# Another order of the experts beside a second block's context, and its stores and input loads on GpSimd's queue

## The chip, the cores and the metric

The kernel runs on one core of a Trainium2 chip. The time is the device time of one execution in microseconds; lower is better.

## The reference

Two blocks stand one behind the other. The first is a hybrid layer on 256 tokens of 1024 features (short convolution, stick-breaking attention and forgetting attention side by side) followed by a mixture of experts: 32 experts, 4 for each token. The second block has two layers (neighbourhood attention, gated linear attention and grouped-query attention, then a feed-forward network) on the 256 tokens of the first block's output and on 256 tokens of a context, which doesn't depend on the first block. All is fp32.

```
logits = (xt @ router_w + router_b).astype(jnp.float32)
top_vals, top_idx = lax.top_k(logits, TOP_K)          # 4 of 32
...
u = xt @ w1 + b1                                       # 1024 -> 2048
glu = jnp.minimum(u[:, ::2], SWIGLU_LIMIT)
lin = jnp.clip(u[:, 1::2], -SWIGLU_LIMIT, SWIGLU_LIMIT)
a = glu * jax.nn.sigmoid(SWIGLU_ALPHA * glu) * (lin + 1)
out = a @ w2 + b2                                      # 1024 -> 1024
return acc + gate_e[:, None] * out.astype(jnp.float32), None
```

## The kernel before

After the first block's mixers and router the kernel sorts the experts by the number of their tokens. A **rank** is a place in that order. A rank has a fixed capacity of rows (`CAPS`, L48): 128 for ranks 0 and 1, 64 for ranks 2 to 17, 32 for ranks 18 to 31. Every expert loads 12 MB of weights, as 12 loads of 1 MB into `m_raw` (5 buffers), all issued by SP at L113: 8 for its first layer (`first`, fp32 matmuls at L904) and 4 for its second (`second`, L962). SP issues the loads in the order of the list `order`, so layer 1 of the next rank is loaded ahead of layer 2 of this one. Between the two layers stand the swiglu (L914 to L921) and a transpose (L929); behind the second, the rows are scattered to the tokens (L1012). `UNITS` (L51) groups ranks whose rows are gathered together (`held`, L845, and `inward`, L863), two groups ahead at a time (`prepare`, L1027).

Beside the experts runs a second stream of work, the **side**. It is a generator: first the rest of the first block's ada layer (L242), then `context` (L1588), which takes the 256 context tokens through the part of the second block that they need: projections, attention (`attend`), the states of the gated linear attention (`gla_states`, which end in sf and sb, L1771) and its output (`gla`), then more projections, the FFN, a norm, and the projections and states of layer 2. Its matmuls run as three passes (L195, L196, L197) on weights split into w_hi (ACT, L96) and w_lo (GpSimd or VectorE, L98); its weights, 0.5 MB apiece, come as `w_raw` over ACT's queue. Its PSUM tiles are named c, two buffers. Tensors that the last part needs are stored to memory by `keep` (L1597), and the context itself is loaded twice as x (L1637, L1642). These stores and loads are issued by SP.

How much of the side stands beside which expert is set while the program is written. The expert loop yields its capacity six times for each rank, and `along` (L1887) gives the side a credit and takes steps of it until the credit is used; the costs of attention and GLA steps are multiplied by `DRY`:

```
SHARE = {128: 0.8, 64: 1.45, 32: 3.2}
DRY = 2.0
...
for step in b.experts(keep):
    b.along(SHARE[step] if step else 1e9)
...
def along(self, c):
    self.credit += c
    while self.credit > 0:
        d = next(self.side, None)
```

After the last expert, `last` runs the second block on the 256 tokens of the first block's output.

Of the kernel before, what the change touches and what calls it, by code (L numbers as in the profile page):

```python
# [17 lines left out]
ALU = mybir.AluOpType  # L18
# [7 lines left out]
NE = 32  # L26
# [11 lines left out]


SHARE = {128: 0.8, 64: 1.45, 32: 3.2}  # L40
DRY = 2.0
FILL = 0.8

FIRST = 2
# [3 lines left out]
CAPS = ((0, 2), 128), ((2, 18), 64), ((18, 32), 32)  # L48
CAP = [n for (lo, hi), n in CAPS for _ in range(lo, hi)]

UNITS = [(u,) for u in range(2)] + [(u, u + 1) for u in range(2, 18, 2)] + [tuple(range(u, min(u + 4, NE))) for u in range(18, NE, 4)]  # L51
FC = 22

MIXED = 2, 3, 4, 5, 0, 1, 6, 7
# [77 lines left out]
class Build:  # L132
# [673 lines left out]
    def experts(self, keep):  # L806
# [3 lines left out]
        nc, tc, io = self.nc, self.tc, self.io  # L810
        with tc.tile_pool(name="m1", bufs=1) as p, tc.tile_pool(name="m2", bufs=2) as p2, \
# [4 lines left out]
            x = keep["x1"]  # L816
# [7 lines left out]
            bl = p.tile([P, 192], F32R, name="bl")  # L824
# [20 lines left out]
            def held(rows, ranks):  # L845

                for t in range(2):
                    for e, r in enumerate(ranks):
                        n = CAP[r]
                        nc.vector.tensor_scalar(rows[:, t, e * n:(e + 1) * n], keep["place"][:, 0:n], keep["rslot"][:, t, r:r + 1],  # L850
                                                None, op0=ALU.is_equal)
# [137 lines left out]
            def biases():  # L989

                for k in range(0, KC, 2):
                    po = ps.tile([P, 512], F32, name="m")
                    for i in range(2):
                        c = (k + i) % 4 * P
                        nc.tensor.matmul(po[:, i * T:(i + 1) * T], b2[k // 4][:, c:c + P], gateT, start=True, stop=True)
                    add(k, po)
                    if k == 2:
                        yield
# [18 lines left out]

            reg = [expert(r) for r in range(NE)]

            order = [(r, layer) for r in (0, 1) for layer in (1, 2)] + [(2, 1)]  # L1020
            for r in range(2, NE):
                order += [(r + 1, 1)] * (r + 1 < NE) + [(r, 2)]
            for r, layer in order:
                w.plan(weights(reg[r], layer), False)
            ready = {}
# [1 line left out]
            def prepare(i):  # L1027

                rows = p2.tile([P, 2, 2 * P], F32R, name="rows", tag="glu", bufs=1)
                xT = p2.tile([P, KC, 2 * P], F32, name="xT", bufs=1)  # L1030
                at = 0
                for ranks in UNITS[i:i + 2]:
                    held(rows[:, :, at:], ranks)
                    for r in ranks:
                        ready[r] = xT[:, :, at:at + CAP[r]]
                        at += CAP[r]

                for z in range(at, 2 * P, 64):
                    nc.vector.tensor_copy(rows[:, :, z:z + 64], rows[:, :, at - 64:at])
                inward(rows, xT)  # L1040


            for c in range(2):
                b1 = p2.tile([P, 512], F32, name="b1", tag="yh")
                nc.scalar.dma_start(b1, io["b_mlp1"][c])
                nc.scalar.activation(b1h[:, c], b1, AF.Copy)
                for q in (slice(32, 64), slice(96, 128)):
                    nc.vector.tensor_tensor(b1h[q, c], b1[q], b1h[q, c].bitcast(F32), op=ALU.subtract)
            prepare(0)
            self.all(rank)  # L1050
            pr.__exit__(None, None, None)
            behind = biases()
            unit = {r: i for i, ranks in enumerate(UNITS) for r in ranks}
            aTs, inside, ys = {}, {}, {}
            for n, (r, layer) in enumerate(order):
                m, ranks = CAP[r], UNITS[unit[r]]
                run = first(m, ready[r], chosen(m, perm[:, r:r + 1])) if layer == 1 else second(m, aTs.pop(r))
# [45 lines left out]
            with tc.tile_pool(name="past", bufs=1) as pf, tc.If(most > 0):  # L1103
# [4 lines left out]
                place = pf.tile([P, 2, P], F32, name="placef")  # L1108
# [8 lines left out]
                with tc.For_i(0, NE, 1) as i:  # L1117
# [12 lines left out]
                    for v in range(2):  # L1130
                        with tc.If(past > v * P):
                            after = w.apart([a for layer in (1, 2) for a in weights(lambda: expert_id, layer)])
# [15 lines left out]
                            u = end(first(128, xT, chosen(128, col[:, 4:5])))  # L1148
# [439 lines left out]
    def context(self, w, ps, tag, saved):  # L1588


        nc, tc, io = self.nc, self.tc, self.io
        one = lambda n: tc.tile_pool(name=n, bufs=1, side="right")
        two = lambda n: tc.tile_pool(name=n, bufs=2, side="right")

        def keep(l, name, t):
            saved[l][name] = tc.dram_tile(list(t.shape), F32, name=f"kept_{name}_{l}")
            nc.sync.dma_start(saved[l][name], t)  # L1597

        def halves(pu):
            return [pu.tile([P, KC, T], F32R, name=n) for n in ("uh", "ul")]  # L1600

        def mixers(l, u, pu, full):
            y = None
            with one("cg") as pg:
                o = {n: pg.tile(sh, F32, name=n) for n, sh in self.GLA_SHAPES + (self.FULL_SHAPES[2:] if full else ())}
                with one("cq") as pq:
                    o.update({n: pq.tile(sh, F32, name=n) for n, sh in self.SHAPES + (self.FULL_SHAPES[:2] if full else ())})
                    done = set()
                    with two("cp") as p2:
                        yield from self.projections(l, 1, u, o, w, p2, ps, tag, full, done)  # L1610
                    for n, _ in self.SHAPES:
                        keep(l, n, o[n])
                    if full:
                        y = halves(pu)
                        with two("ca") as p2:
                            yield from dry(self.attend(self.units(l, 1, o, None, done), *y, p2, ps, tag, done))
                with one("cl1") as p, two("cl2") as p2:
                    for n in ("sf", "sb"):
                        o[n] = p.tile([P, 64], F32, name=n)
                    yield from dry(self.gla_states(o, p2, ps, tag))  # L1620
                    for n in ("sf", "sb"):
                        keep(l, n, o[n])
                    if full:
                        yield from dry(self.gla(l, 1, o, None, *y, p, p2, ps, tag, done))
            return y

        def dry(steps):

            for c in steps:
                yield c and c * DRY  # L1630

        mod = [m[:, 1] for m in self.mod2]
        with one("cu") as pu:
            u = halves(pu)
            with one("cx") as px, two("ct") as p2:
                x = px.tile([P, KC, T], F32, name="x")
                nc.sync.dma_start(x, io["ctx"])  # L1637
                yield from self.modulated(x, mod[0][:, 0:8], mod[0][:, 8:16], u, p2)
            y = yield from mixers(0, u, pu, True)
            with one("cx") as px:  # L1640
                x = px.tile([P, KC, T], F32, name="x")
                nc.sync.dma_start(x, io["ctx"])  # L1642
                for k in range(0, KC, 2):
                    nc.gpsimd.tensor_scalar(x[:, k:k + 2], x[:, k:k + 2], ALPHA, None, op0=ALU.mult)
                for i in range(2):
                    with one("cf") as p:
                        acc = p.tile([P, KC, T], F32, name="acc")
                        if i == 0:
                            for ks in MIXED2:
                                yield from self.columns(acc, lambda k: (y[0][:, k], y[1][:, k]), ks, MIXED2[0][0], MIXED2[-1][1], w, ps, tag)  # L1650
                        else:
                            u = halves(pu)
                            with one("ch") as p1, two("ch2") as p2:
                                yield from self.modulated(x, *self.affine(mod[0], 1, 0, 0, p1), u, p2, None, normed)
                                self.settle(x, normed[0], 0, 0, p1)
                                yield from self.ffn(u, w, acc, p1, p2, ps, tag)
                        with two("cr2") as p2:
                            chunk, finish = self.norm(acc, mod[0][:, 24 * i + 16:24 * i + 24], x, px, p2, ps, tag)
                            for k in range(KC):
                                chunk(k)  # L1660
                                yield 0.4
                            normed = finish()
                            yield 1.8
                u = halves(pu)
                with two("ct") as p2:
                    yield from self.modulated(x, *self.affine(mod[1], 0, 0, 1, px), u, p2, None, normed)
                yield from mixers(1, u, pu, False)
# [410 lines left out]
```

## Time and profile before

| | |
|---|---|
| median of three runs | 2369.41 us (2366.2 to 2372.82) |
| profiled execution | 2358.65 us, span 2357.0 us |
| TensorE busy | 2144.4 us, 91% of the span |
| VectorE, ScalarE, GpSimd busy | 46%, 37%, 24% |
| moved by DMA | 667.36 MB, mean 283 GB/s |
| expert stretch | about 279 to 1587 us |

The span is that of one profiled execution; the median is of other executions. Busy time is the time in which an engine works on an instruction, without issuing. The DMA share of a stretch is the mean busy share of the core's 16 DMA engines.

### The profile page before, as it was taken

What the parts mean: (1) busy time and instruction counts of PE and PEld (TensorE: products, weight loads), DVE (VectorE), ACT (ScalarE), POOL (GpSimd) and SP (SyncE); (2) the same over time, 40 slices, a digit from 0 to 9 for tenths busy, and PEclk for the clock granted to TensorE, in tenths of its full rate; (3) what the DMA queues carried; (4) which work ended last, traced back from release to release, by engine and by line L of the source; (5) the groups of instructions that cost most, each with busy time, mean ns of one, the idle gap of its engine ahead of it and who ended that gap; (6) DMA issues with size and microseconds to landing.
All of it is one profiled execution on the core that took longest, in us unless ns stands there. A gap on an engine that the chain in (4) does not pass through costs nothing. (4 is left out here: it accounts for less than half of the span.)

```text
span 2357.0 us, 38285 instructions
## 1 busy us (share of the span) xinstructions
PE 2144.4 (91%) x15238; PEld 1503.0 (64%) x15239; DVE 1087.7 (46%) x2146; ACT 862.6 (37%) x1585; POOL 567.6 (24%) x335
## 2 busy tenths in 40 slices
PE   7899799999999988977999998968989999899998
PEld 4667533455444433524776765637879997788997
DVE  4765333221334322325443345227569767757434
ACT  2533201132232111213333333314555555466554
POOL 1001100122100000202444442504214443322442
PEclk8999799999999999977998999979999999999999
DMA  9867657899988899998999999993256754233553
GB/s 369 316 236 278 262 193 253 334 393 366 368 315 305 326 403 416 378 393 331 377 379 397 374 409 366 395 371 118 82 189 247 275 183 146 90 104 112 190 186 101
DMA packets 121721, 667.36 MB, mean 283 GB/s; under 512 B 14944, under 2 KB 16864, under 8 KB 62784
## 3 DMA queue, kind: packets, MB, share of 16 engines
q1 hardware_dynamic: 104016, 597.86, 67.5%
q10 hardware_dynamic: 17520, 66.99, 7.6%
q8 instruction: 122, 2.00, 0.3%
q14 instruction: 63, 0.52, 0.1%
HBM read 661.51 MB, written 3.28 MB: 282 GB/s over the span
## 5 line engine op out<-in xcount | busy, mean ns | idle before, releaser
L98 POOL TENSOR_TENSOR w_lo<-w_raw,w_hi 128x1024 fp32r<-128x1024 f32 x210 | 503.9, 2403 | 1098.8 <-ACT w_hi L96 890.1
L96 ACT ACTIVATE w_hi<-w_raw 128x1024 fp32r<-128x1024 f32 (+1 forms) x332 | 346.1, 1048 | 418.4 <-PE c L196 162.1
L904 PE MATMUL u<-m_raw,xT 128*64 128x512 f32 (+1 forms) x2048 | 396.0, 620 | 28.2 <-DMA m_raw<-in_w_mlp 28.2
L195 PE MATMUL ps<-uh,w_hi 128*128 128x256 f32 (+1 forms) x944 | 274.0, 291 | 10.4 <-ACT uh L1214 6.0
L197 PE MATMUL ps<-uh,w_lo 128*128 128x256 f32 (+1 forms) x944 | 270.5, 287 | 4.9 <-DVE w_lo L98 3.2
L196 PE MATMUL ps<-ul,w_hi 128*128 128x256 f32 (+1 forms) x944 | 270.7, 287 | 1.3 <-DVE ul L1215 1.2
L904 PEld LDWEIGHTS u<-m_raw,xT 128*64 128x64 f32 (+1 forms) x2048 | 103.8, 127 | 220.9 <-issue 172.5
L962 PE MATMUL y<-m_raw,aT 128*32 128x256 f32 (+1 forms) x1536 | 216.0, 507 | 19.1 <-DMA m_raw<-in_w_mlp 16.3
L98 DVE TENSOR_TENSOR w_lo<-w_raw,w_hi 128x1024 fp32r<-128x1024 f32 (+1 forms) x122 | 153.0, 1254 | 110.5 <-ACT w_hi L96 109.8
L195 PEld LDWEIGHTS ps<-uh,w_hi 128*128 128x128 f32 (+1 forms) x944 | 182.2, 193 | 17.7 <-ACT uh L1214 7.1
L197 PEld LDWEIGHTS ps<-uh,w_lo 128*128 128x128 f32 (+1 forms) x944 | 182.7, 194 | 5.9 <-DVE w_lo L98 3.9
L196 PEld LDWEIGHTS ps<-ul,w_hi 128*128 128x128 f32 (+1 forms) x944 | 183.0, 194 | 2.9 <-DVE ul L1215 2.0
L195 PE MATMUL c<-uh,w_hi 128*128 128x256 f32 (+1 forms) x584 | 172.0, 295 | 4.2 <-ACT uh L1214 3.1
L196 PE MATMUL c<-ul,w_hi 128*128 128x256 f32 (+1 forms) x584 | 170.7, 292 | 0.0
L197 PE MATMUL c<-uh,w_lo 128*128 128x256 f32 (+1 forms) x584 | 170.5, 293 | 0.0
L195 PE MATMUL ps<-hh,w_hi 128*128 128x256 f32 x560 | 163.8, 293 | 0.0
L197 PE MATMUL ps<-hh,w_lo 128*128 128x256 f32 x560 | 159.1, 284 | 1.2 <-DVE w_lo L98 1.2
L196 PE MATMUL ps<-hl,w_hi 128*128 128x256 f32 x560 | 159.4, 285 | 0.5 <-DVE hl L189 0.5
L962 PEld LDWEIGHTS y<-m_raw,aT 128*32 128x32 f32 (+1 forms) x1536 | 74.3, 129 | 131.8 <-issue 89.5
L914 DVE TENSOR_SCALAR glu<-u 128x512 f32<-128x512 f32 (+1 forms) x34 | 23.3, 687 | 236.4 <-PE u L904 236.3
L195 PEld LDWEIGHTS c<-uh,w_hi 128*128 128x128 f32 (+1 forms) x584 | 112.8, 193 | 25.1 <-issue 15.7
L196 PEld LDWEIGHTS c<-ul,w_hi 128*128 128x128 f32 (+1 forms) x584 | 113.2, 194 | 13.6 <-issue 10.9
(554 smaller groups left out, 3921.4 us busy)
## 6 DMA issues: line engine op xcount, KB each, us to landing
m_raw<-in_w_mlp SPq DMA_DIRECT2D x384, 1024.0 KB, 8.0
f_raw<-in_w_ada SPq DMA_DIRECT2D x47, 1024.0 KB, 7.1
w_raw<-in_w_ffn_in SPq DMA_DIRECT2D x88, 512.0 KB, 4.2
w_raw<-in_w_in SPq DMA_DIRECT2D x64, 512.0 KB, 5.0
w_raw<-in_w_ffn_in ACTq DMA_DIRECT2D x44, 512.0 KB, 8.6
w_raw<-in_w_ffn_out SPq DMA_DIRECT2D x44, 512.0 KB, 4.2
w_raw<-in_w_in ACTq DMA_DIRECT2D x34, 512.0 KB, 7.9
g_raw<-in_w_ada SPq DMA_DIRECT2D x16, 1024.0 KB, 8.4
```

Source lines behind the costliest of these rows:

```text
L96: nc.scalar.activation(hi, r, AF.Copy)
L98: e.tensor_tensor(lo, r, hi.bitcast(F32), op=ALU.subtract)
L195: nc.tensor.matmul(out, lh, rh, start=start, stop=False)
L196: nc.tensor.matmul(out, lh, rl, start=False, stop=False)
L197: nc.tensor.matmul(out, ll, rh, start=False, stop=stop)
L904: nc.tensor.matmul(u[z][r:r + s], xT[:, k, x0:x0 + s], ws[k - k0][:, c * 512:(c + 1) * 512], start=False, stop=k == KC - 2)
L914: nc.vector.tensor_scalar(glu, u0, 7.0, None, op0=ALU.min)
L962: nc.tensor.matmul(y[z][r:r + s], a[:, k], ws[(k - k0) // 2][:, k % 2 * D + c * wd:k % 2 * D + (c + 1) * wd], start=k == 3, stop=k == 4)
```

## The change

The ranks are taken in another order: eight ranks of 32 rows (18 to 25), then the two of 128, the sixteen of 64, and the last six of 32 (26 to 31). The list `order` is built from that. Ahead of a rank of 128 rows, and behind ranks 0 and 1, no layer is loaded early. Since a 32-row rank comes first, the tile `bl` is set to zero once. `DRY` is 2.4 instead of 2.0. The twelve stores of `keep` and the two loads of x are issued by GpSimd.

```diff
-DRY = 2.0
+DRY = 2.4
...
-UNITS = [(u,) for u in range(2)] + [(u, u + 1) for u in range(2, 18, 2)] + [tuple(range(u, min(u + 4, NE))) for u in range(18, NE, 4)]
+UNITS = [tuple(range(u, u + 4)) for u in (18, 22)] + [(u,) for u in range(2)] + [(u, u + 1) for u in range(2, 18, 2)] + [(26, 27, 28, 29), (30, 31)]
...
-            order = [(r, layer) for r in (0, 1) for layer in (1, 2)] + [(2, 1)]
-            for r in range(2, NE):
-                order += [(r + 1, 1)] * (r + 1 < NE) + [(r, 2)]
+            turn = [r for ranks in UNITS for r in ranks]
+            order = []
+            for r, after in zip(turn, turn[1:] + [None]):
+                if not order or r in (0, 1, 2):
+                    order.append((r, 1))
+                order += [(after, 1)] * (after is not None and r not in (0, 1) and CAP[after] < 128) + [(r, 2)]
...
+            if CAP[turn[0]] == 32:
+                nc.vector.tensor_scalar(bl, keep["place"][:, 0:192], 0.0, None, op0=ALU.mult)
             prepare(0)
...
         def keep(l, name, t):
             saved[l][name] = tc.dram_tile(list(t.shape), F32, name=f"kept_{name}_{l}")
-            nc.sync.dma_start(saved[l][name], t)
+            nc.gpsimd.dma_start(saved[l][name], t)
...
                 x = px.tile([P, KC, T], F32, name="x")
-                nc.sync.dma_start(x, io["ctx"])
+                nc.gpsimd.dma_start(x, io["ctx"])
```

In SP's program of the kernel before, the stores of the two states sf and sb of the context's first layer stand between loads of expert weights (each load has a register instruction, ISA, ahead of it):

```order
L113 ISA
L113 DMA m_raw<-in_w_mlp 128x2048
L113 ISA
L113 DMA m_raw<-in_w_mlp 128x2048
L1597 DMA kept_sf_6574<-sf 128x64
L1597 DMA kept_sb_6576<-sb 128x64
L113 ISA
L113 DMA m_raw<-in_w_mlp 128x2048
```

In GpSimd's program of the changed kernel the stores of that layer (line 1602 there) stand among the splits of the context's weights, and those of sf and sb between the last of these and the first work of the context's `gla`:

```order
L98 TENSOR_TENSOR w_lo<-w_raw,w_hi 128x1024 x7
L1602 DMA kept_nav_4007<-nav 128x768
L98 TENSOR_TENSOR w_lo<-w_raw,w_hi 128x1024 x3
L1602 DMA kept_nak_4005<-nak 128x768
L1602 DMA kept_sf_5080<-sf 128x64
L1602 DMA kept_sb_5082<-sb 128x64
L1828 TENSOR_TENSOR gl_e<-gl_B 128x128
L1829 TENSOR_TENSOR gl_e<-gl_C 128x128
```

So these stores no longer wait for SP's loads ahead of them, but for the work ahead of them on GpSimd.

On TensorE, a stretch among the 64-row ranks of the kernel before holds the experts' own work alone, without passes of the context (L195 to L197):

```order
L929 MATMUL m<-ident,sg 128x128 x4
L894 MATMUL u<-b1h,bl 128x512
L904 MATMUL u<-m_raw,xT 64x512 x32
L894 MATMUL u<-b1h,bl 128x512
L962 MATMUL y<-m_raw,aT 64x512 x8
L929 MATMUL m<-ident,sg 128x128 x4
```

In the changed kernel all the ranks of 64 rows have such passes between their matmuls; here is a piece of one:

```order
L1012 MATMUL m<-selT,yh 128x256
L1012 MATMUL m<-selT,yl 128x256
L196 MATMUL c<-ul,w_hi 128x256
L197 MATMUL c<-uh,w_lo 128x256
L195 MATMUL c<-uh,w_hi 128x256
L196 MATMUL c<-ul,w_hi 128x256
L904 MATMUL u<-m_raw,xT 64x512 x8
L197 MATMUL c<-uh,w_lo 128x256
```

The 32-row ranks of the kernel before have the passes of the context between theirs:

```order
L195 MATMUL c<-hh,w_hi 128x256
L196 MATMUL c<-hl,w_hi 128x256
L904 MATMUL u<-m_raw,xT 32x512 x8
L197 MATMUL c<-hh,w_lo 128x256
L195 MATMUL c<-uh,w_hi 128x256
L196 MATMUL c<-ul,w_hi 128x256
```

In the changed kernel the last of the context on TensorE is the end of its second layer's states (L1773 there), in rank 26; behind it the last 32-row ranks stand alone:

```order
L1773 MATMUL c<-glv,gs_d 128x256 x4
L904 MATMUL u<-m_raw,xT 32x512 x24
L962 MATMUL y<-m_raw,aT 32x256 x16
L929 MATMUL m<-ident,sg 128x64 x4
L894 MATMUL u<-b1h,bl 128x512 x2
L962 MATMUL y<-m_raw,aT 32x256 x16
L904 MATMUL u<-m_raw,xT 32x512 x32
```

The context's work has moved from the 32-row ranks at the end to the ranks of 32 rows at the start and to those of 64.

## Rows read from the trace of the kernel before

**Rows 1.** The page: span, and busy time and share of each engine.

```profile
span 2357.0 us, 38285 instructions
PE 2144.4 (91%) x15238; PEld 1503.0 (64%) x15239; DVE 1087.7 (46%) x2146; ACT 862.6 (37%) x1585; POOL 567.6 (24%) x335
```

**Rows 2.** Windows: us, width, busy of PE, PEld, DVE, ACT, POOL; clock; DMA; GB/s.

```profile
279.00:419.00 140.00, 131.54 (x606) 48.74 (x607) 44.67 (x155) 17.63 (x36) 0.90 (x4) 0.97 0.59 211
359.00:419.00 60.00, 55.06 (x266) 21.72 (x264) 19.31 (x52) 12.64 (x26) 0.43 (x2) 1.00 0.65 233
419.00:637.00 218.00, 214.90 (x1225) 115.96 (x1222) 50.42 (x102) 57.12 (x102) 49.60 (x21) 1.00 0.97 376
620.00:804.00 184.00, 172.64 (x956) 81.62 (x956) 77.11 (x207) 53.83 (x138) 8.68 (x15) 0.99 0.87 319
804.00:962.00 158.00, 138.19 (x688) 55.66 (x688) 34.65 (x70) 23.87 (x39) 5.24 (x5) 0.99 0.99 403
868.00:928.00 60.00, 51.53 (x243) 18.16 (x241) 12.50 (x25) 6.83 (x11) 0.00 (x0) 0.97 1.00 408
1007.00:1037.00 30.00, 21.54 (x118) 7.78 (x110) 5.22 (x8) 4.28 (x6) 4.68 (x2) 0.72 1.01 408
1120.00:1541.00 421.00, 390.35 (x3324) 285.81 (x3316) 171.43 (x297) 151.44 (x252) 179.14 (x76) 0.96 0.98 386
1541.00:1587.00 46.00, 30.66 (x230) 13.65 (x234) 9.83 (x25) 3.67 (x7) 0.00 (x0) 0.73 0.92 372
2200.00:2300.00 100.00, 100.00 (x838) 100.00 (x838) 40.17 (x65) 54.44 (x83) 42.53 (x18) 1.00 0.56 182
```

**Rows 3.** DMA issues in 419:637, 620:804, 804:962, 1120:1541 (KB each, us to landing).

```profile
m_raw<-in_w_mlp SPq DMA_DIRECT2D x69, 1024.0 KB, 8.1
m_raw<-in_w_mlp SPq DMA_DIRECT2D x54, 1024.0 KB, 6.4
m_raw<-in_w_mlp SPq DMA_DIRECT2D x59, 1024.0 KB, 7.9
m_raw<-in_w_mlp SPq DMA_DIRECT2D x122, 1024.0 KB, 9.3
```

**Rows 4.** Timeline of PE: start, us, instructions of a 64-row and a 32-row rank.

```profile
899.74 3.65 PE L904 MATMUL u<-m_raw,xT 128*64 128x512 f32 x16
...
1504.92 1.93 PE L962 MATMUL y<-m_raw,aT 128*32 128x256 f32 x32
```

**Rows 5.** Windows of line L195 alone: width, PE, PEld, clock, DMA, GB/s.

```profile
419.00:637.00 218.00, 48.63 (x168) 30.95 (x168) 1.00 0.97 376
1120.00:1541.00 421.00, 170.79 (x582) 112.34 (x582) 0.96 0.98 386
```

**Rows 6.** Instructions of L1872, the end of GLA: ns, first and last start.

```profile
L1872 PE MATMUL c<-gl_A,glv x16: 272/273/323, 798.4 to 803.3; 128*64 128x128 f32 x16
```

**Rows 7.** Tile sf, the timeline of SP and ACT, and POOL's waits.

```profile
L1771 DVE COPY sf<-c x8: 212/220/230, 729.6 to 1584.3; 32x64 f32<-32x64 f32 x8
...
932.42 0.43 SPq L1597 DMA_DIRECT2D kept_sf<-sf  x1
932.90 0.43 SPq L1597 DMA_DIRECT2D kept_sb<-sb  x1
...
941.05 1.09 ACT L1477 ACTIVATE acc<-c 128x512 f32<-128x512 f32 x2 [12.28 <-DMA kept_sb<-sb]
...
POOL ss L1543 <- DMA kept_sb<-sb: 163.5, 1, 163.5
```

**Rows 8.** Waits of POOL, the second load of x: total us, times, longest.

```profile
POOL x L1644 <- DMA x<-in_ctx: 47.3, 1, 47.3
```

**Rows 9.** Timeline of ACT near the end of the last experts.

```profile
1580.56 0.60 ACT L1756 ACTIVATE gs_d<-c 128x512 f32<-128x512 f32 x1 [6.44 <-DMA kept_gav<-gav]
```

**Rows 10.** Timeline of DVE: the selection of a group's rows.

```profile
401.18 1.39 DVE L850 TENSOR_SCALAR rows<-place,rslot 128x64 fp32r<-128x64 f32 x8
```

**Rows 11.** The page's costliest groups: GpSimd's splits (busy us, mean ns, idle before).

```profile
L98 POOL TENSOR_TENSOR w_lo<-w_raw,w_hi 128x1024 fp32r<-128x1024 f32 x210 | 503.9, 2403 | 1098.8 <-ACT w_hi L96 890.1
```

More of the change, by code (lines that the diff above doesn't have):

```diff
@@ L1641, in context @@
                 x = px.tile([P, KC, T], F32, name="x")
-                nc.sync.dma_start(x, io["ctx"])
+                nc.gpsimd.dma_start(x, io["ctx"])
                 for k in range(0, KC, 2):
```

## The prediction, made before the changed kernel ran

> **What bounds the kernel now.** I read the page first: the span and TensorE's share [rows 1] say that TensorE works most of the time, but that is a mean over stretches with different limits. So I cut the expert stretch, 279 to 1587 us (1308 us), into windows [rows 2] and counted the 1 MB expert loads issued in four of them [rows 3]. Width divided by loads is the price of one load, and there are 384 in all (32 experts of 12). The reader is to see that this price follows from what stands beside the load:
> - 419 to 637, 64-row experts with projections of the context: 218 / 69 = 3.16 us a load, TensorE 214.9 of 218 busy, DMA 0.97. Both are nearly full.
> - 620 to 804, 64-row experts with the context's attention and GLA: 184 / 54 = 3.41 us; TensorE 172.6 busy, DMA 0.87.
> - 804 to 962, 64-row experts with no context work: 158 / 59 = 2.68 us, DMA 0.99 at 403 GB/s. Loads set the pace. In 868 to 928, with 408 GB/s and share 1.00, one MB (1.0486 million bytes) is 2.57 us.
> - 1120 to 1541, 32-row experts with the context's projections and FFN: 421 / 122 = 3.45 us, DMA 0.98, TensorE 390 of 421.
>
> The experts' own matmuls come from the timeline [rows 4]: 16 records of 64 rows serve two loads in 3.65 us, 1.83 us a load (21.9 a rank); 32 records of 32 rows serve two loads in 1.93, 0.96 a load. A 128-row expert has twice the matmuls of a 64-row one, about 3.65 a load. A projection matmul is 100 / 838 = 0.119 us (window 2200 to 2300 [rows 2], TensorE full). Row counts at L195 times three, for the three passes, give the projections per load [rows 5]: 168 x 3 / 69 = 7.3 in the first window, 582 x 3 / 122 = 14.3 in the last. What is left of TensorE's time in 419 to 637 (gathers, scatters, biases) is 214.9 - 69 x 1.83 - 504 x 0.119 = 28.6, or 0.41 a load.
>
> Why did 804 to 962 have no context work? GLA ended at 803 [rows 6]. The copies of the states sf and sb were done soon after 729, but SP issued their stores at 932, behind the m_raw loads ahead of them in its program [rows 7]. The next tile, acc, lies where sb lay, so GpSimd and ACT waited for the store of sb, until 941. The context stood still for 137 us. In the same way its second load of x kept GpSimd waiting 47.3 us [rows 8], and the last state work of the context ran at 1580, 6.44 us behind the store of gav [rows 9], at the very end, where only two experts' loads were left to hide it.
>
> **The change part by part.** In the order of the changed kernel's instructions the loads and the context's work fall into six stretches. A: ranks 18 to 20, 44 loads (the first rank opens with two first layers), 492 projection matmuls and the rest of the ada layer. B: ranks 21 to 23, 36 loads, attention and GLA, 45 projections. C: ranks 24 and 25, 16 loads, 159 projections and a norm. D: the two of 128 rows, 24 loads, 142 projections. E: ranks 2 to 17, 200 loads, 1731 projections, 8.66 a load. F: the last six, 64 loads, no context work but the tail of the last states. The sum is 384.
>
> *A.* Projections per load are 11.2, close to 1120 to 1541, so I take 3.45: 44 x 3.45 = 152. By parts, rank 18 starts as rank 0 did before (140 of the window 279 to 419 less 60 for rank 1, the window 359 to 419, leaves 80), less its smaller blocks (12 x 2.7 = 32), plus 156 x 0.119 = 19: 67 against 20 x 3.45 = 69. The longer opening (sixteen selections of rows instead of four) is 12 x 0.17 = 2 us, from eight in 1.39 [rows 10].
>
> *B.* Beside 54 loads, attention and GLA took 184 us, of which 54 x 1.83 = 99 were the experts' blocks, so the chain's own part is 85. Now 36 loads of 0.96 = 35 go with it, and 45 x 0.119 = 5: 125 if the work packs, against 36 x 2.68 = 96 if loads alone bound it and 184 if the chain's own dependences did. It is nearest to the packed sum, since TensorE was busy 172.6 of 184; I take 130.
>
> *C.* 12 x 3.45 + 4 x 2.68 = 52, and 8 for rank 25's second layer, which no first layer follows, with the norm beside it: the window 1541 to 1587 lost 46 - 12 x 2.68 = 14 in such a place (0 to 14; I take about half). C is 60.
>
> *D.* Rank 1 took 60 with TensorE 55 busy; two of them, 120. The 142 projections (17 us) stand where the ada layer stood.
>
> *E.* TensorE per load: 1.83 + 0.41 + 8.66 x 0.119 = 3.27. At the busy share of 419 to 637 (0.986) it is 3.32: 664. Bounds: 200 x 3.16 = 632 (no dearer than in that window) and 200 x 3.45 = 690 (as the dearest loads). I take 664, the row nearest in kind.
>
> *F.* TensorE needs 0.96 + 0.41 = 1.37 a load, loads 2.57 to 2.68: 64 x 2.6 = 166, plus 2 for the end. A lower clock would not decide here: 1007 to 1037 has a granted clock of 0.72 (part of it at 1.2 and not 2.4 GHz), TensorE 21.5 of 30 busy and DMA still 1.01 [rows 2].
>
> *Stores and input loads.* 14 DMAs leave SP for GpSimd. SP wins 14 x 0.43 = 6 us of issuing [rows 7], hidden under its loads and counted at nothing. On GpSimd the trace has no issue to price: between 0.43, as on SP, and 2.4, its dearest usual instruction [rows 11], so 6 to 34 us of a queue that was busy 179 of 421 us at its fullest [rows 2]. I take nothing on the path; if GpSimd became late, w_lo would be next and TensorE's third pass behind it. GpSimd's next work behind the stores of sf and sb in the program is GLA's gl_e, so a store that waits for the state copies holds that up, by the time of the copies, 0.2 us each [rows 7]. What it gives is that the context doesn't stop after GLA. That is worth little by itself: with a stop of 137 us as before, 41 loads of E would run at 2.68 instead of 3.32 (-26), and their 355 projections, 15 loads of 0.5 MB, would come into F, at 386 GB/s for 20 us, with a tail at the end that costs 14 as in 1541 to 1587: +8 in all. DRY 2.4 charges attention more, so B holds 36 loads rather than fewer; it has no cost of its own.
>
> Sum: 152 + 130 + 60 + 120 + 664 + 168 = 1294, against 1308: -14, and +2 for the opening: -12. What follows (1587 to the end) is not touched. The profiled execution of before took 2358.65, so 2347; the median of the runs, 2369.41, is 1.0046 times that, so **2357**.
>
> **A page's rule against the row.** The stores' delay was 202 us from the copy (730) to the issue (932), and only 8 from the issue to the end of ACT's wait (941) [rows 7], so it was SP's program order. The Trainium skill, DMA: Bandwidth & Descriptors, section Issuing engines are not separate DMA queues, says that transfers share the same 16 engines whoever issues them, and that several issuers save only the sequencer's issuing time. By it the move gives only the 6 us of issuing, which nothing waits for, and the stop stays. The row disagrees as far as the blocked queue goes.
>
> **The rivals.**
> 1. *Slower: attention and GLA don't compress.* The chain of B runs through DVE, ACT and two PSUM banks; if it keeps 184 us beside fewer loads, B is +54: 2347 + 54 = 2401, times 1.0046 = 2411. For: DMA was 0.87 there, so something other than loads was slow. Against: TensorE was 94% busy. From B = 142 it eats the whole gain, from 149 it makes the kernel slower.
> 2. *No change: the stretches without context work only change places.* Before, 59 + 12 loads ran without it, afterwards the 64 of F. If E runs at 3.38 a load (TensorE 0.967 busy, between the 0.986 and 0.927 of the two projection windows), 12 us are gone: 2359, times 1.0046 = 2370. The other way to it: the stores land late wherever they are issued, and the stop stays: the +8 above gives 2355, times 1.0046 = 2366. The rows of the store speak against that, and the TensorE rows leave the first open. The rule above would give this second case.
> 3. *More gain:* B at its 96 and E at 632 are 66 less, 2281, times 1.0046 = 2291; half of that, 2325.
>
> **How the numbers follow.** A measurement of this kernel can tell about 0.3%, 7 us, from no change. The forecast has 0.43; more gain 0.12; no change 0.20 (0.05 of it with the stores late); slower 0.25 (0.15 from B, 0.10 from E above 3.41). So faster is 0.55, same 0.20, slower 0.25. The range takes in half of rival 3 and half of rival 1 (B at 157, +27: 2347 + 27 = 2374, times 1.0046 = 2385) and E at 690 (+26: 2373, 2384): **2320 to 2390**; what is left out is under 2 in 10. The likeliest case alone reaches from 2343 to 2364.
>
> **What would show it.** Right: stores of sf and sb issued within 10 us of their copies; no stop of the context after GLA; A about 153 to the end of rank 20's loads, B about 130 with TensorE over 0.9 busy; E near 3.32 a load with DMA about 0.95; F at 2.6 a load with DMA 0.99 or more, and no context work at the end. Wrong: B over 150; TensorE in E under 0.96 busy with idle time behind w_lo or a PSUM bank; or projections left in F.

## The result and the profile after

The changed kernel takes 2398.69 us (median of four runs, 2391.65 to 2406.01) against 2367.8 for the kernel before, run beside it (2364.38 to 2372.82). The ratio is 1.0144, with a 95% interval of 1.0107 to 1.018 (the two medians alone give 1.013): it is slower by some 31 us. The prediction was 2357, range 2320 to 2390, and slower had a chance of 0.25.

First the page of the changed kernel: its span, the engines' busy time, and the granted clock in 40 slices of 60 us.

```profile
span 2401.4 us, 38297 instructions
...
PE 2191.0 (91%) x15238; PEld 1524.1 (63%) x15239; DVE 1101.6 (46%) x2147; ACT 862.9 (36%) x1585; POOL 573.9 (24%) x349
...
PEclk7999889976999999999999998778999999999999
```

Against [rows 1] the span is 44.4 us longer, and TensorE is busy 46.6 us longer with the same 15238 instructions. So in these two executions the same matmuls took longer, and TensorE's idle time is all but the same (212.6 and 210.4 us). The two slices from 480 to 600 us have a granted clock of 0.7 and 0.6.

Next the windows of the changed kernel, one for each of the prediction's stretches A to F, and below two of 10 us inside B. The columns are those of [rows 2].

```profile
281.00:441.00 160.00, 151.19 (x1156) 94.47 (x1154) 58.27 (x157) 44.56 (x78) 50.89 (x28) 0.95 0.93 370
441.00:598.00 157.00, 140.70 (x890) 74.03 (x886) 68.29 (x180) 48.51 (x130) 17.57 (x27) 0.76 0.72 271
598.00:657.00 59.00, 53.25 (x439) 37.28 (x435) 28.38 (x50) 18.17 (x30) 20.00 (x13) 0.94 0.90 340
657.00:786.00 129.00, 121.69 (x639) 57.12 (x631) 43.91 (x93) 30.55 (x59) 12.43 (x5) 0.97 0.66 231
786.00:1464.00 678.00, 657.50 (x3832) 375.36 (x3829) 219.70 (x402) 183.22 (x298) 180.97 (x79) 0.99 0.94 364
1464.00:1634.00 170.00, 110.26 (x843) 43.29 (x841) 33.83 (x75) 15.00 (x28) 1.07 (x2) 0.78 0.96 391
480.00:490.00 10.00, 10.00 (x57) 5.01 (x49) 3.04 (x9) 2.62 (x9) 0.00 (x0) 0.50 0.61 229
550.00:560.00 10.00, 9.90 (x48) 5.85 (x47) 4.89 (x13) 0.89 (x2) 1.67 (x4) 0.50 0.63 243
```

| stretch | forecast | measured |
|---|---|---|
| A, ranks 18 to 20 (44 loads) | 152 and 2 for the opening | 160 |
| B, ranks 21 to 23 (36), attention and GLA | 130 | 157 |
| C, ranks 24 and 25 (16) | 60 | 59 |
| D, the two of 128 rows (24) | 120 | 129 |
| E, the sixteen of 64 rows (200) | 664 | 678 |
| F, the last six (64) | 168 | 170 |
| sum | 1296 | 1353 |

Of the 57 us that the sum missed, B has 27, E 14, D 9 and A 6. In B the granted clock is 0.76, and in the two short windows 0.50, TensorE's lower level (1.2 of 2.4 GHz), although by its records it was busy for 10.00 and 9.90 of 10 us. In the kernel before the same attention and GLA stood beside 64-row experts, with a clock of 0.99 [rows 2]. In B, half the clock doubles an expert's block; this is PE's timeline of the changed kernel, and the like block of [rows 4] took 1.93 us:

```profile
492.91 3.64 PE L962 MATMUL y<-m_raw,aT 128*32 128x256 f32 x32
```

The stores did what was forecast. The instructions of the tile sf in the changed kernel show the first copy at 529.7 and GpSimd's store at 531.1, where before there were 202 us between them [rows 7]; an issue on GpSimd takes 0.54 us, near the lower bound that the prediction gave it (0.43).

```profile
L1776 DVE COPY sf<-c x8: 204/220/229, 529.7 to 1478.8; 32x64 f32<-32x64 f32 x8
L1602 POOL DMA_DIRECT2D kept_sf<-sf x2: 537/538/538, 531.1 to 1479.4; - x2
```

And yet this part turned out to cost time, as the experiments show.

### The profile page after: what moved, and what is told of

It reads as the page before. It is cut to its first block, busy times and chain, and to the rows that moved or that the text cites. A ratio compares the mean times of both kernels' runs of the same rounds, so it can differ in the third digit from the quotient of the medians.

```text
span 2401.4 us, 38297 instructions
## 1 busy us (share of the span) xinstructions
PE 2191.0 (91%) x15238; PEld 1524.1 (63%) x15239; DVE 1101.6 (46%) x2147; ACT 862.9 (36%) x1585; POOL 573.9 (24%) x349
## 3 DMA queue, kind: packets, MB, share of 16 engines
q0 software_dynamic: 928, 4.33, 0.5%
## 5 line engine op out<-in xcount | busy, mean ns | idle before, releaser
L904 PE MATMUL u<-m_raw,xT 128*64 128x512 f32 (+1 forms) x2048 | 410.7, 658 | 32.5 <-DMA m_raw<-in_w_mlp 32.5
L195 PE MATMUL ps<-uh,w_hi 128*128 128x256 f32 (+1 forms) x944 | 274.9, 292 | 9.7 <-ACT uh L1219 6.5
L197 PE MATMUL ps<-uh,w_lo 128*128 128x256 f32 (+1 forms) x944 | 271.1, 287 | 3.9 <-DVE w_lo L98 3.2
L195 PEld LDWEIGHTS ps<-uh,w_hi 128*128 128x128 f32 (+1 forms) x944 | 183.0, 194 | 16.8 <-ACT uh L1219 7.3
L197 PEld LDWEIGHTS ps<-uh,w_lo 128*128 128x128 f32 (+1 forms) x944 | 183.5, 194 | 5.0 <-DVE w_lo L98 3.9
L195 PE MATMUL c<-uh,w_hi 128*128 128x256 f32 (+1 forms) x584 | 170.1, 292 | 4.2 <-ACT uh L1219 1.6
L197 PE MATMUL c<-uh,w_lo 128*128 128x256 f32 (+1 forms) x584 | 170.1, 292 | 0.0
L195 PE MATMUL ps<-hh,w_hi 128*128 128x256 f32 x560 | 164.2, 293 | 0.0
L197 PE MATMUL ps<-hh,w_lo 128*128 128x256 f32 x560 | 159.4, 285 | 1.2 <-DVE w_lo L98 1.2
L195 PEld LDWEIGHTS c<-uh,w_hi 128*128 128x128 f32 (+1 forms) x584 | 110.8, 190 | 19.4 <-issue 9.0
L197 PEld LDWEIGHTS c<-uh,w_lo 128*128 128x128 f32 (+1 forms) x584 | 110.6, 190 | 18.3 <-issue 15.6
```

The lines of the kernel that those rows point to most:

```text
L195: nc.tensor.matmul(out, lh, rh, start=start, stop=False)
L197: nc.tensor.matmul(out, ll, rh, start=False, stop=stop)
L904: nc.tensor.matmul(u[z][r:r + s], xT[:, k, x0:x0 + s], ws[k - k0][:, c * 512:(c + 1) * 512], start=False, stop=k == KC - 2)
```

## The experiments

Three theories were held against each other. The **clock theory**: attention and GLA beside 32-row experts let the clock fall, and B's 27 us are that. The **queue theory**: GpSimd's queue, or the DMAs made by its software (the page of the changed kernel has a queue `software_dynamic` that moved 4.33 MB, and that of the kernel before has none), hold things up. After the first four runs the queue theory got a rival, the **place theory**: the queue matters because without a stop other projections come to stand beside 64-row ranks. All ratios are to the kernel before, run beside each kernel on the same chip.

### One part alone: the queues

Edit, to the kernel before:

```diff
-            nc.sync.dma_start(saved[l][name], t)
+            nc.gpsimd.dma_start(saved[l][name], t)
...
-                nc.sync.dma_start(x, io["ctx"])
+                nc.gpsimd.dma_start(x, io["ctx"])
...
-                nc.sync.dma_start(x, io["ctx"])
+                nc.gpsimd.dma_start(x, io["ctx"])
```

> The kernel before with only its 12 stores and 2 loads of the context moved to GpSimd's queue. Clock theory (the changed kernel is slow because attention and GLA beside 32-row experts let TensorE's granted clock fall to 0.76 in 441 to 598 us, against 0.99 beside 64-row experts before): the clock of the attention stretch stays at 0.98 or more, and the time is the kernel before's, from -10 to +2 us. Queue theory (GpSimd, which stood 84 us at the store of sf in the changed kernel, and its software-made DMAs hold up the context): slower than before by 10 us or more.

Measured: 2383.84 us against 2363.02, ratio 1.0097 (1.0072 to 1.0122). The queues alone cost 21 to 23 us, as the queue theory had it, and the clock beside attention is not their cause: in the stretch of attention and GLA (621 to 802 us) it was 1.00. Where they cost it, the windows show, ranks 11 to 17 and then 18 to 31. (The profiled execution was the fastest of its kernel, 13.6 us longer than that of the kernel before, so it shows a part of the loss.) First the kernel before:

```profile
803.00:1038.00 235.00, 205.49 (x1084) 90.19 (x1080) 57.39 (x120) 39.22 (x60) 19.40 (x11) 0.96 0.97 392
1038.00:1587.00 549.00, 481.38 (x3989) 333.62 (x3989) 219.78 (x401) 179.69 (x308) 197.11 (x89) 0.92 0.96 380
```

Then the run with the queues moved:

```profile
802.00:1096.00 294.00, 280.21 (x1647) 161.21 (x1645) 107.84 (x207) 84.90 (x147) 75.11 (x41) 0.98 0.92 351
1096.00:1601.00 505.00, 414.27 (x3467) 263.26 (x3465) 169.17 (x319) 134.57 (x225) 145.56 (x66) 0.91 0.97 392
```

The same line L195 alone (first pass of each projection) in these windows, before and with the queues moved:

```profile
803.00:1038.00 235.00, 18.39 (x64) 12.04 (x64) 0.96 0.97 392
1038.00:1587.00 549.00, 184.66 (x624) 122.05 (x624) 0.92 0.96 380
```

```profile
802.00:1096.00 294.00, 67.64 (x233) 44.43 (x233) 0.98 0.92 351
1096.00:1601.00 505.00, 132.19 (x455) 86.69 (x455) 0.91 0.97 392
```

(233 - 64) x 3 = 507 projection matmuls have moved from the 32-row ranks to the 64-row ranks 11 to 17. There they cost 294 - 235 = 59 us, 0.116 each, which is TensorE's own price of 0.119; what they had cost beside 32-row ranks was 549 - 505 = 44 us, 0.087 each. (The prices are rough: 56 other records of the context moved along.) The difference, 15 us, is that of these two executions. TensorE went from 205.5 of 235 busy to 280.2 of 294, and DMA from 0.97 to 0.92. TensorE's program is another one in this run: the passes of the context stand beside other ranks in it. So the stop of 137 us after GLA in the kernel before was no loss: while it lasted, loads ran at full rate, and the projections were made up where TensorE had room.

### The other part alone: order and DRY

Edit, to the changed kernel: the same three lines back to `nc.sync`.

> The changed kernel (new order of ranks and DRY 2.4) with the 14 DMAs issued by SP as before. Clock theory: as slow as the changed kernel, within 10 us of it, with the clock below 0.85 in the stretch of attention and GLA. Queue theory: faster than the changed kernel by 20 us or more, near the kernel before.

Measured: 2371.83 against 2363.02, ratio 1.0042 (1.002 to 1.0063). Each theory is half right: the clock is 0.78 in the stretch of attention and GLA (450 to 598 us), as the clock theory said, but most of the loss is gone, as the queue theory said. 1.0042 x 1.0097 = 1.0139, against 1.0144 for both together: the two parts add up.

The queue's part is seen best in F. First the last six ranks of this run, then line L195 alone in them:

```profile
1435.00:1604.00 169.00, 123.53 (x1038) 62.15 (x1036) 40.12 (x69) 29.33 (x51) 21.85 (x9) 0.87 1.00 408
1435.00:1604.00 169.00, 18.22 (x64) 12.03 (x64) 0.87 1.00 408
```

With the stores on SP the context stops on its way, and 64 x 3 = 192 of its projections come into F, which takes 169 us with them and took 170 without. Where TensorE is full they would cost 192 x 0.119 = 23 us by estimate, and the two ratios lie 24 us apart.

### The order, with attention beside more rows

Edit, to the changed kernel:

```diff
-CAPS = ((0, 2), 128), ((2, 18), 64), ((18, 32), 32)
+CAPS = ((0, 2), 128), ((2, 18), 64), ((18, 20), 32), ((20, 24), 64), ((24, 32), 32)
...
-UNITS = [tuple(range(u, u + 4)) for u in (18, 22)] + [(u,) for u in range(2)] + [(u, u + 1) for u in range(2, 18, 2)] + [(26, 27, 28, 29), (30, 31)]
+UNITS = [(u, u + 1) for u in range(18, 26, 2)] + [(u,) for u in range(2)] + [(u, u + 1) for u in range(2, 18, 2)] + [(26, 27, 28, 29), (30, 31)]
...
-                    yield step
+                    yield 32 if r > 17 else step
...
-                yield m
+                yield 32 if r > 17 else m
```

> The changed kernel with a capacity of 64 rows instead of 32 for ranks 20 to 23, beside which most of attention and GLA runs; the result of the computation is unchanged, 48 loads get 0.87 us of TensorE work more each at full clock, 42 us. Clock theory: the clock beside ranks 21 to 23 comes back to 0.95 or more, the added work is paid back by it, and the time is within 12 us of the changed kernel. Theory of a bound by TensorE's work or by the chain of attention, whatever the clock: slower than the changed kernel by 30 to 42 us.

Measured: 2392.69 against 2363.02, ratio 1.0123 (1.0094 to 1.0152), no slower than the changed kernel's 1.0144. Windows of this run beside ranks 21, 22, 23 and 24; the first three have 64 rows, the last 32:

```profile
467.00:506.00 39.00, 37.81 (x176) 15.79 (x172) 14.87 (x36) 12.96 (x38) 2.86 (x2) 1.00 0.92 361
506.00:545.00 39.00, 37.86 (x214) 16.40 (x212) 17.32 (x48) 12.79 (x39) 0.00 (x0) 1.00 0.89 323
545.00:589.00 44.00, 40.09 (x252) 20.37 (x251) 20.48 (x55) 15.48 (x39) 3.84 (x8) 0.92 0.78 291
589.00:633.00 44.00, 40.61 (x319) 25.72 (x320) 22.20 (x58) 11.00 (x22) 7.86 (x15) 0.81 0.82 300
```

With 64-row blocks the clock is back (1.00, 1.00 and 0.92; the last is short of the 0.95 expected), and beside the 32-row rank it falls to 0.81, with GLA running on. The three ranks of 64 rows, with about twice the matmul time for the expert, took 39 to 44 us where the changed kernel's ranks 21 to 23 took 157 / 3 = 52 on average; attention and GLA are spread over four ranks here and over three there, so the ranks aren't to be compared one by one, but the total is. The added 42 us of TensorE's work raised its busy time by only 15 (2205.9 against 2191.0). This is the clock theory's result. Which of the instructions beside the 32-row ranks the clock answers to, no run separates.

### The order, with four ranks of 32 first

Edit, to the changed kernel:

```diff
-UNITS = [tuple(range(u, u + 4)) for u in (18, 22)] + [(u,) for u in range(2)] + [(u, u + 1) for u in range(2, 18, 2)] + [(26, 27, 28, 29), (30, 31)]
+UNITS = [(18, 19, 20, 21)] + [(u,) for u in range(2)] + [(u, u + 1) for u in range(2, 18, 2)] + [(22, 23, 24, 25), (26, 27, 28, 29), (30, 31)]
```

> The changed kernel with four ranks of 32 rows first instead of eight (ten at the end instead of six), so that attention and GLA fall beside the two ranks of 128 and ranks 2 to 4 of 64. Clock theory: the clock there is 0.95 or more, and by prices per load the expert stretch takes about 1307 us instead of 1352, the time 2345 to 2375 us. If the attention's own chain or the full TensorE of the 64-row ranks with projections costs the time, it stays within 10 us of the changed kernel.

Measured: 2368.43 against 2363.02, ratio 1.0025 (1.0003 to 1.0047): 1.2% less than the changed kernel. Attention and GLA now stand beside the ranks of 128 and ranks 2 to 4:

```profile
464.00:725.00 261.00, 250.00 (x1297) 109.43 (x1299) 90.73 (x235) 58.41 (x140) 7.37 (x16) 0.98 0.75 278
```

The clock is 0.98 there, and TensorE's busy time over the span falls from 2191.0 to 2161.5. The expert stretch ended at 1604 us, 16 later than the prices per load gave.

### Is it GpSimd, or the place of the projections?

Edit, to the kernel before: the three lines with `nc.scalar` (ACT's queue).

> The kernel before with the 14 DMAs issued by ACT instead of GpSimd; TensorE's program is that of the run with GpSimd's queue alone (no stop of the context after GLA, 699 projection matmuls beside ranks 11 to 17 where the kernel before has 192). Place theory (the queue's cost of some 20 us is that projections come beside 64-row ranks, where TensorE is nearly full, instead of 32-row ranks, where loads set the pace and TensorE has room): as slow as that run, 14 to 25 us over the kernel before. GpSimd theory (the cost is GpSimd's blocked queue or its software-made DMAs): within 5 us of the kernel before.

Measured: 2384.78 against 2366.6, ratio 1.0082 (1.0055 to 1.0109). The same as on GpSimd, so neither GpSimd's waits nor its DMAs are the cause: in the run with GpSimd's queue it stood 126 us for the copies of sf, and here ACT stood at most 4.8 us ahead of the first one (from 740.4 to its issue at 745.2). Ranks 11 to 17 took 295 us here.

Edit, to the run with the queues alone:

```diff
-            nc.gpsimd.dma_start(saved[l][name], t)
+            (nc.sync if name in ("sf", "sb") else nc.gpsimd).dma_start(saved[l][name], t)
```

> The kernel before with 10 of the 14 DMAs on GpSimd, but the stores of sf and sb (both layers) on SP again, so that the context stops after GLA as before (no projections beside ranks 12 to 14; 268 beside ranks 11 to 17). Place theory: within 8 us of the kernel before. GpSimd theory: the blocked wait at sf goes and with it part of the cost, but ten software-made DMAs stay: still 10 us or more over the kernel before.

Measured: 2369.11 against 2366.6, ratio 1.0014 (0.9995 to 1.0033). Four of the fourteen DMAs, those of sf and sb, carry the cost of the queues. With them on SP the first store of sf comes at 941.8 us again, after a copy at 738.7; the context stands still from 831 to 951, and the loss is gone.

```profile
L1597 SPq DMA_DIRECT2D kept_sf<-sf x2: 331/334/336, 941.8 to 1588.6; - x2
```

### Orders with the stores on SP

Edit, to the four-first order: the three lines back to `nc.sync`.

> Four ranks of 32 rows first, DRY 2.4, all 14 DMAs on SP: attention and GLA beside the ranks of 128 and 64 rows (clock theory: granted clock 0.95 or more there), and the context stops twice beside 64-row ranks, so that some 650 projections instead of 1580 stand beside ranks 2 to 17 and the rest beside 32-row ranks. Clock and place theory together: 10 to 25 us faster than the same order with GpSimd's queue (2368), so 2343 to 2358, and faster than the kernel before. If the place of projections doesn't matter: as that run, within 5 us.

Measured: 2347.8 against 2366.6, ratio 0.992 (0.9891 to 0.9949). The count in the expectation was off: 1388 projections stood beside ranks 2 to 17 on GpSimd's queue, 653 on SP's. The two ratios are 0.0105 apart, 25 us; for 735 projections that is 0.034 each, near 0.116 - 0.087 = 0.029.

Edit, to that kernel:

```diff
-UNITS = [(18, 19, 20, 21)] + [(u,) for u in range(2)] + [(u, u + 1) for u in range(2, 18, 2)] + [(22, 23, 24, 25), (26, 27, 28, 29), (30, 31)]
+UNITS = [(18, 19)] + [(u,) for u in range(2)] + [(u, u + 1) for u in range(2, 18, 2)] + [tuple(range(u, u + 4)) for u in (20, 24, 28)]
```

> Two ranks of 32 rows first, DRY 2.4, all 14 DMAs on SP; attention and GLA beside ranks 3 to 7, only about 480 projections beside the sixteen 64-row ranks, about 1870 beside twelve 32-row ranks at the end, 13 a load. Clock and place theory: clock 0.95 or more beside attention, 2340 to 2360 us, within 10 us of the four-first order on SP and not slower than the kernel before.

Measured: 2342.51 against 2366.6, ratio 0.99 (0.9876 to 0.9923), the fastest kernel of the study. (320 projections stand beside its 64-row ranks, not 480.) Its windows: attention and GLA, then ranks 8 to 17, then the twelve ranks of 32.

```profile
519.00:770.00 251.00, 235.38 (x1287) 116.18 (x1285) 89.36 (x230) 69.44 (x163) 18.64 (x19) 0.97 0.86 320
770.00:1102.00 332.00, 279.91 (x1412) 112.87 (x1412) 79.43 (x167) 48.68 (x77) 25.44 (x15) 0.95 0.97 394
1102.00:1572.00 470.00, 432.85 (x3683) 314.69 (x3681) 197.65 (x358) 169.63 (x290) 190.83 (x85) 0.96 0.97 387
```

The clock stays up beside attention, loads run at 394 GB/s beside 64-row ranks, and TensorE is 92% busy beside the last ranks, with no stretch of F's kind (65% busy).

### The third part alone: DRY

Edits: `DRY = 2.4` in the kernel before; and `DRY = 2.0` in the two-first order on SP.

> The kernel before with DRY 2.4 instead of 2.0 alone. In TensorE's program the stop after GLA is longer (no projections beside ranks 12 to 16, 168 beside rank 17), so that 192 stand beside ranks 11 to 17, as many as in the kernel before. Place theory, at 0.03 us for each projection moved between 64-row and 32-row ranks (59 less 44 us for 507 of them in the run with GpSimd's queue alone): the same time, within 6 us. If DRY were the change's hidden cost: 10 us or more over the kernel before.

Measured: 2346.96 against 2367.72, ratio 0.9913 (0.9881 to 0.9944).

> The two-first order on SP with DRY 2.0 instead of 2.4: some 530 projections instead of 320 stand beside ranks 2 to 17. Place theory: 209 x 0.03 = 6 us slower than with DRY 2.4 (2342.5), 2344 to 2353. If the place doesn't matter: the same time.

Measured: 2365.22 against 2367.72, ratio 0.9994 (0.997 to 1.0017), so some 22 us slower than with 2.4.

Both misses are of one kind: DRY 2.4 gains 20 us in either order, and the count of moved projections gives 0 and 6. Windows of ranks 18 to 31 with DRY 2.4 in the order of before:

```profile
1037.00:1574.00 537.00, 470.47 (x3981) 326.66 (x3978) 215.37 (x394) 178.86 (x308) 197.72 (x90) 0.94 0.98 392
```

and of ranks 20 to 31 in the two-first order with DRY 2.0, to be read beside the last window of the two-first order above:

```profile
1110.00:1589.00 479.00, 424.88 (x3461) 297.96 (x3460) 175.12 (x316) 147.91 (x246) 171.03 (x72) 0.90 0.94 372
```

The first has the same 624 rows of L195 as the kernel before in 1038 to 1587, but 11 us less busy TensorE, at a clock of 0.94 instead of 0.92, and DMA 0.98 instead of 0.96 (the windows are one execution of each). The second has 70 rows of L195 fewer than the window with DRY 2.4 (554 and 624), that is 25 us less work at 0.119, but only 8 us less busy time, at 0.90 instead of 0.96. So a part of DRY's gain is again the clock beside 32-row experts. Over all runs, too, the mean granted clock was 0.956 to 0.960 with DRY 2.4 alone against 0.946 to 0.957 for the kernel before, and in the two-first order 0.958 to 0.964 against 0.949 to 0.960.

Another part is place within the 32-row ranks. Here is rank 30 alone, in the kernel before and with DRY 2.4:

```profile
1541.00:1574.00 33.00, 22.50 (x160) 9.21 (x160) 7.58 (x16) 2.96 (x6) 0.00 (x0) 0.72 0.97 398
```

```profile
1527.00:1561.00 34.00, 30.92 (x299) 21.43 (x291) 11.86 (x18) 9.71 (x16) 13.58 (x6) 1.00 1.02 424
```

In the kernel before the context is through by 1529 us, but for its last states, and rank 30 stands alone. With DRY 2.4 rank 30 has 39 rows of L195, 117 projections, and takes 1 us more, not 117 x 0.087 = 10. In return ranks 18 to 20 have 33 rows of L195 instead of 105 and take 107 us instead of 123. The two-first order agrees: rank 30 took 34 us with 117 projections and 31 without. So 0.087 is a mean over ranks in which a projection costs next to nothing and ranks in which TensorE is full, and the counts, which priced all 32-row ranks alike, could not see this. These are single executions; how DRY's gain divides between clock and place was not separated.

## Why the prediction was wrong

The change has three parts that work against each other. DRY alone is 0.9913; order and DRY 1.0042, so the order on top of DRY is 1.0042 / 0.9913 = 1.013; the queues on top of both 1.0144 / 1.0042 = 1.010. (DRY was not run alone in the changed order, so this split goes by the order in which the parts are added.)

- **B, the step that failed most.** It summed parts at durations read where the clock was 0.96 or more (attention and GLA beside 64-row experts, the expert's blocks beside projections) and took it for granted that they hold where attention and GLA stand beside 32-row experts. At those durations TensorE had 106 us of work in B: 172.6 - 54 x (1.83 + 0.41) = 52 for attention and GLA, 36 x (0.96 + 0.41) = 49, and 5 for 45 projections. Its records show 140.7. The 34 us between are the clock: 106 / 0.76 = 140. The prediction looked at the clock in one place only, F, where it decides nothing (0.78 measured, and F took 170 against 168), and left it out where TensorE bounds the time. The run with 64 rows for ranks 20 to 23 shows this cause, and the four-first order agrees.
- **Stores and input loads.** Their working had 8 us to gain from losing the stop, and the queues as nothing on the path. Measured, the stop is worth some 20 us to have. The mis-sized piece is 41 loads of E at 2.68 against 3.32, 26 us; in the run with the queues alone 84 loads beside ranks 11 to 17 went from 2.80 to 3.50 each, and what the 32-row ranks won back by losing the projections was less (59 against 44). So a gain of 8 us for taking the stop away came out as a loss of some 20. The prediction was right on the mechanism, SP's program order: the store came 1.4 us after its copy.
- **E** was 678 against 664, mis-sized by 14. TensorE's work per load, 657.5 / 200 = 3.29, was right (3.27); its busy share was 0.970 and not the 0.986 of a shorter window, as rival 2 had it (0.967).
- **D** was 129 against 120: the 142 projections were counted at nothing, as standing where the ada layer stood, but that was a wrong reading: in 359 to 419, the window that D was taken from, the ada layer (L242) kept TensorE busy for 1.06 us. TensorE was busy 121.7 us in D, against twice 55.1 in that window. **A** was 160 against 154, with a clock of 0.95. **C** and **F** were right.
- **DRY** was given no cost and no gain of its own; it gains 20 us in the order of before.
- **The page's rule.** By the Trainium skill, DMA: Bandwidth & Descriptors, section Issuing engines are not separate DMA queues, starting DMAs on several engines at once saves only the time that the sequencer takes to start them. No run here shows that time to matter, and the runs on GpSimd's and ACT's queue agree with each other (ratios 1.0097 and 1.0082). But against SP the queue did matter, by where in an engine's program a store stands; that the stop stays, which the prediction drew from the rule, was not so.
- **The rivals.** B at 157 lies behind the 149 from which rival 1 has the kernel slower, but by another mechanism than the chain of attention that it named: TensorE was 90% busy, at a lower clock. Rival 2's E came true on top of it. The two together, and D, go beyond the range, which held each alone. (Rival 1's 2401 times 1.0046 is 2412 and not 2411, which changes nothing.)

One more step lay ahead of the sum: projections were taken to cost TensorE's 0.119 or a load's share, whichever bounds, but no term asked where each projection is cheapest. The order of the changed kernel puts 1731 of them beside 64-row ranks, where TensorE is full, and none beside the last six, where it is busy 110 of 170 us and where the run with order and DRY shows 192 of them to cost nothing.

## What to carry to other kernels

A duration of TensorE read in one stretch holds in another only if the granted clock holds, so read the clock column of a stretch before pricing work that moves, and ask what stands beside it there. When two streams are woven, price a moved piece in both places: a stall that shifts work from a stretch where TensorE is full to one where loads set the pace can be a gain, and taking it away a loss. Parts of a change that look like details (here a factor of 2.4 for 2.0, and four small stores) are to be run alone.

## What the hardware showed that was not expected

TensorE's granted clock was 0.50 in a window where its records leave no idle time (10.00 of 10 us busy, 480 to 490 us); the engine ran 32-row fp32 blocks, transposes of 128 columns, scatters and attention's matmuls there. With 64-row blocks beside the same kind of work it was 1.00 (467 to 545 us of the run with 64 rows).

Over the eleven kernels profiled here without the padding to 64 rows, TensorE's busy time went from 2133.7 (two-first order on SP) to 2191.0 us (the changed kernel) with 15238 matmul records in each.

A DMA issued by GpSimd took it 0.54 us (the two stores of sf in the changed kernel), and one by SP 0.33 and 0.43 (the same two in the kernel before).
